# Masked self-attention over sequences of mixed length: waits for older loops moved into skip branches, and GpSimd's casts reading their row masks from the table

## The chip, the cores and the metric

The kernel runs on one NeuronCore of one Trainium2 chip. The metric is the device time of one execution in microseconds. One execution has been recorded by the hardware profiler; all times "from the span's start" below are from that record.

## The reference

Thirty-two sequences of up to 512 tokens (the lengths are drawn between 64 and 511) with 512 features go through one self-attention layer with 8 heads of 64 features. What lies behind a sequence's length stays zero in the output.

```
for b in range(batch):
    seq_len = lengths[b]
    x_b = x[b, :seq_len].copy()
    qkv = np.matmul(x_b, w_qkv)
    q, k, v = np.split(qkv, 3, axis=-1)
    ...
    scores = scale * np.matmul(q, k.transpose(0, 2, 1))
    scores_max = np.max(scores, axis=-1, keepdims=True)
    attn = np.exp(scores - scores_max)
    attn = attn / (np.sum(attn, axis=-1, keepdims=True) + 1e-08)
    out_b = np.matmul(attn, v).transpose(1, 0, 2).reshape(seq_len, dim)
    output[b, :seq_len] = out_b
```

## The kernel before

**Sorting and loops.** The sequences are sorted by length on the chip and taken in 16 pairs, longest first. There is one loop for each padded length N of 512, 448, 384, 352, 320, 288, 256, 224, 192, 160, 128 and 96 (LOOPS). A loop runs over the pairs whose longer member fits N and not the next smaller one; the register end_v says at which pair it stops. A loop with no pair is passed over by the compare-and-branch at its entry (L1477); a loop that has run a pair goes back, or on, at L1497. One pass through a body handles one pair in two *positions*, j = 0 and j = 1, so that the run has 32 positions, 0 to 31.

**A position.** While the attention of one sequence is computed, the next sequence is projected. In position p TensorE does the scores of sequence p (s, L1123), its weighted sums (a, L1207), and the Q, K and V projections of sequence p+1 (q and k L261, v L272). ScalarE takes the exponentials of the scores (L1137) and some copies out of PSUM. VectorE takes the other copies (L1165, L1181), and behind each group of weighted sums three operations: R, the reciprocal of the row sums (L1217, reads PSUM), U, which multiplies it by the row mask in the spare column of v_aug or in the tile queries (L1223, both inputs in SBUF), and O, the division into the output tile (L1226, reads PSUM). O0, O2, O4, O6 are the divisions of the heads from 0, 2, 4, 6 on; in the widest loops there is one for every head.

**Input and masks.** The input of a sequence runs ahead of its projection. In position p SyncE loads x of sequence p+5 in float32 (LD, L1006), and GpSimd casts sequence p+3 to float16 and blanks the rows behind its length (C: one tensor_tensor multiply at L319 for each tile of 128 rows, x times a mask column broadcast along the row). SyncE then transposes that result by DMA (XT, L289) into xT, from which the projections of position p+2 read. The float32 buffers, the float16 buffers and xT are rings of two, taken by parity, so that C of position p writes the buffer that XT of position p-2 reads. The mask for C is made on VectorE: operation M (pair_mask, L968) copies the row of the table alive that belongs to the sequence, at an address from a register, into the tile mask (m_bufs), also a ring of two. Behind M on VectorE stands L (L1044), which writes the spare column of v_aug for the next sequence from alive, and, in loops whose last tile is at most half full, for that tile from a second table, lower. In these loops GpSimd also gathers the half tiles of two sequences (Y, L1066), and at the entry of a loop it may clear columns of kT (E, L1302) or half a tile of v_aug (Z, L1310).

**Order.** The order of the steps in each position is written out by hand in ORDER, in short names: P stands for M and C, D for LD, L, S for scores and exponentials, K, Q, V for projections with their copies (a star puts the copy on ScalarE), A for weighted sums with R, U and O, X for XT. Each engine runs its own part of that list in order, and positions follow one another without a barrier.

**Waits.** plan_waits walks through every chain of loops that can occur (the head, then a loop; a loop u, then a loop v) and gives each operation the waits it needs: a semaphore per operation name, which counts its executions, against a constant or a register. A register named pos, iter or rare grows with each pass; posin, iterin and rarein are set at a loop's entry (L1468 and L1470 to L1475); end_v is worked out in the head from the loops' ends. A wait is an instruction of its own where it doesn't ride on the operation (L1418). A loop that follows on its direct predecessor may need fewer waits than one that follows on a loop further back, when those between have been passed over. In the kernel before these waits stand in the loop's body all the same, and are carried out whether loops were passed over or not; posold is a register that keeps an older entry's value for them.

**The head.** Ahead of the loops stand the sort, the tables, the first two sequences' cast and projections, the weights' casts, and idle matmuls on a tile of ones ("warm") between them.

Of the kernel before, what the change touches and what calls it, by code (L numbers as in the profile page):

```python
# [14 lines left out]
ALU = mybir.AluOpType  # L15
AX = mybir.AxisListType

P = 128
# [17 lines left out]
def plan_waits(head, bodies, entries, rare):  # L36
# [13 lines left out]

    waits = defaultdict(list)
    has = [{op.name for j in range(2) for op in body[j]} for body in bodies]
    shared = set().union(*has)

    def follow(chain):
# [5 lines left out]
        for at, v in enumerate(chain):  # L64
# [10 lines left out]
            for w, j, k, op in todo:  # L75
# [13 lines left out]
                for wait in waits[w, j, k]:  # L89
                    got = [  # L90
                        o
                        for o in seen[wait[1]]
                        if wait[0] in ("last", "entry", "head", "lead")
                        or (wait[0] == "pos" and o["b"] == b - wait[2])
                        or (wait[0] == "iter" and o["b"] // 2 == b // 2 - wait[2])
                        or (wait[0] == "posin" and o["b"] == first - wait[2])
                        or (wait[0] == "posold" and older and o["b"] == first - wait[2])
                        or (wait[0] == "iterin" and o["b"] // 2 == first // 2 - wait[2])
                    ]
                    if got:  # L100
                        learn(got[-1])
# [5 lines left out]
                for o in sorted(needs, key=lambda o: -o["order"]):  # L107
                    if mine[o["by"]] >= o["count"]:
                        continue
                    before = o["b"] < first  # L110
                    if o["entry"]:
                        wait = ("entry", o["name"])
                    elif o["name"] not in shared:
                        wait = ("head", o["name"])
                    elif v == "head":
                        wait = ("lead", o["name"])
                    elif before and o["name"] in rare:
                        wait = ("iterin", o["name"], first // 2 - o["b"] // 2)
                    elif o["name"] in rare:
                        wait = ("iter", o["name"], b // 2 - o["b"] // 2)  # L120
                    elif o["dma"] and before:
                        wait = ("iterin", o["name"], first // 2 - o["b"] // 2)
                    elif o["dma"]:
                        wait = ("iter", o["name"], b // 2 - o["b"] // 2)
                    elif o["name"] not in has[v]:
                        wait = ("last", o["name"])
                    elif before:
                        wait = ("posold" if older else "posin", o["name"], first - o["b"])
                    else:
                        wait = ("pos", o["name"], b - o["b"])  # L130
                    waits[w, j, k].append(wait)
                    learn(o)
                by = op.name if op.dma else op.eng
                count = (seen[by][-1]["count"] if seen[by] else 0) + 1
                after = dict(mine)
# [14 lines left out]
    for v in range(len(bodies)):  # L150
# [1 line left out]
        for u in reversed(range(v)):  # L152
            follow([u, v, v])
        follow(["head", v, v])
    return waits, has


@with_exitstack
def kernel(
# [170 lines left out]
    def before_loops():  # L330
# [280 lines left out]
        fetch("x1.0", 1, 1, 0, 0, NT // 2)  # L611
        fetch("x1.2", 1, 1, 0, NT // 2, NT)

        warm("warm1", ones16, 16, 1, ())

        more = small(
            "more",
# [164 lines left out]
        def twos(source):  # L782
# [50 lines left out]
        )  # L833
        joined("table", four, computed, 20, ("four", "computed"), table)
        op(
            "M",
            "DVE",
            lambda: dve.tensor_scalar(
                out=m_bufs[0], in0=alive[:, 2, :], scalar1=0.0, scalar2=None, op0=ALU.add
            ),  # L840
            ("alive",),
            ("m0",),
        )
        op(
            "L",
            "DVE",
            lambda: dve.tensor_scalar(
# [44 lines left out]

        def casts():
            for t in range(NT):
                last = cast(0, t, nc.gpsimd)
            return last

        op("C", "POOL", casts, ("xn0", "m0"), ("x160", *(f"x160.{t}" for t in range(NT))))
        op("zeros", "POOL", lambda: pool.memset(zeros, 0.0), (), ("zeros",))
        fetch("LD0", 1, 1, 2, 0, NT)  # L900
        op(
# [10 lines left out]
        op("joinPE", "PE", lambda: None, [f"xT1.{t}" for t in range(NT)], [f"bk{k}" for k in (2, 4, 5, 6)])  # L912
        op("joinACT", "ACT", lambda: None, [f"et{e}" for e in range(4)])
        op("joinSP", "SP", lambda: None, ("zeros", "table"))
        op("joinDVE", "DVE", lambda: None, ("lower",), ["m1"])
        op("joinPOOL", "POOL", lambda: None, [f"xT1.{t}" for t in range(NT)], [f"x161.{t}" for t in range(NT)])
        return ops

# [29 lines left out]
    def position(N, j, at, ring):  # L948
# [15 lines left out]
        def op(*args, **kw):  # L964
            ops.append(Op(*args, **kw))

        def pair_mask():
            return nc.vector.tensor_scalar(  # L968
                out=m_bufs[o],
                in0=alive[:, bass.ds(at("DVE") + (j + 3), 1), :].rearrange("p o t -> p (o t)"),  # L970
                scalar1=0.0,
                scalar2=None,
                op0=ALU.add,
            )

        def casts():
            for t in range(n):
                last = cast(o, t, nc.gpsimd)
            return last

        def numbers(pair, handles):
# [265 lines left out]
        for step in steps(N, j):  # L1247
            kind, act = step[0], step.endswith("*")
            num = int(step.strip("*")[1:] or 0)
            if kind == "P":  # L1250
                op("M", "DVE", pair_mask, (), (f"m{o}",))
                op("C", "POOL", casts, (f"xn{o}", f"m{o}"), (f"x16{o}",))
                if half_last and j == 0:
                    for b in (1, 0):
                        op(f"Y{b}", "POOL", lambda b=b: gathered(b), (f"xT{b}",), ("lastT",))
# [61 lines left out]
    def at(eng):  # L1317
        return here[eng]
# [5 lines left out]
    entries = [entry(N) for N in LOOPS]  # L1324
    head = before_loops()
    rare = {"Y0", "Y1", "w", "W0", "W1"}
    waits, has = plan_waits(head, bodies, entries, rare)

    def op_of(v, j, k):
        return head[k] if v == "head" else (entries[v] if j is None else bodies[v][j])[k]  # L1330

    lead = defaultdict(int)
    awaited = set()
    for key, todo in waits.items():
        for wait in todo:
            if wait[0] == "head":
                awaited.add(wait[1])
# [24 lines left out]
    def value_of(v, j, wait):  # L1362
# [5 lines left out]
            return "pos", lead[name] + 1 - wait[2] + j  # L1368
        if wait[0] == "iter":
            return f"iter{unit(name)}", unit(name) * (lead[name] + 1 - wait[2])  # L1370
        if wait[0] in ("posin", "posold"):
            return wait[0], lead[name] + 1 - wait[2]
        if wait[0] == "iterin":
            return f"iterin{unit(name)}", unit(name) * (lead[name] + 1 - wait[2])
        if wait[0] == "lead":
# [5 lines left out]


    raised = {"pos": 2, "rare": 1, "iter16": 16, f"iter{16 * NT}": 16 * NT}
    entered = {"posold": 0, "posin": 2, "rarein": 1, "iterin16": 16, f"iterin{16 * NT}": 16 * NT}

    wanted = defaultdict(set)
    fixed = defaultdict(set)
    for (v, j, k), todo in waits.items():
        op = op_of(v, j, k)
        for wait in todo:  # L1390
            base, amount = value_of(v, j or 0, wait)
            if base:
                wanted[op.eng].add((base, amount))
                if base in entered:
                    fixed[v, op.eng].add((base, amount))
                if base == "posold":
                    wanted[op.eng].add(("posin", amount))
                    fixed[v - 1, op.eng].add(("posin", amount))

    def emit(v, j, k, op):  # L1400
        if not op.skip:
# [27 lines left out]
    with tc.tile_critical():  # L1429
# [32 lines left out]

        for v, N in enumerate(LOOPS):
            for e, eng in EN.items():
                for base, amount in sorted(fixed[v, e], key=lambda f: (f[0] != "posold", f)):
                    reg = regs[e][base, amount]
                    if base == "posold":
                        eng.reg_mov(reg, regs[e]["posin", amount])  # L1468
                        continue
                    eng.reg_mul(reg, rare_pair if base == "rarein" else pair, entered[base])  # L1470
                    eng.reg_add(reg, reg, amount)
            for k, op in enumerate(entries[v]):
                emit(v, None, k, op)
            for e in final:
                EN[e].reg_sub(final[e], of(ends[v], e), 1)  # L1475
            body, after = f"loop_{N}", f"after_{N}"
            nc.br_lt(pair, ends[v], on_true=body, on_false=after)  # L1477
            with nc.body(body):
                hints = {}
# [59 lines left out]
```

## Time and profile before

| what | value |
|---|---|
| median of 3 runs | 343.71 us (343.44 to 344.86) |
| profiled execution | 343.52 us |
| its span, first to last instruction | 341.7 us |
| VectorE's mask copies (L968) | 32, 5.5 us |
| GpSimd's casts (L319) | 85 tiles, 86.3 us |
| TensorE's granted clock, mean | 0.995 |

The profile counts an engine as busy while it executes; register, branch and semaphore instructions are not counted, and appear with a q behind the engine's name (PEq, DVEq; PEldq for TensorE's, in the views by line). In the groups by line, "x" is the count, then come the busy time in us and the mean duration in ns, and after the second bar the engine's idle time just before these instructions with what ended most of it. In views of one line, three numbers divided by slashes are minimum, median and maximum in ns. In the timeline a row has start and duration in us, engine, line, operation, output and input, count, and in brackets the idle time ahead of it. In the chain of work a row has start, length and name. A row of the windows has the stretch, its length, then the busy time and count for each engine, TensorE's clock, the DMA share and GB/s. A matmul's weight load (PEld) is a row of its own.

In the profiled execution the loops' first scores start at these times (us): 512 at 22.2, 448 at 60.8, 384 at 95.9, 352 at 121.8, 320 at 195.6, 288 at 218.9, 256 at 241.9, 224 at 257.1, 192 at 284.9, 160 at 297.3, 128 at 321 (first matmuls at 322.84), 96 at 330.9. Each row of the profile before can be placed in its loop by them.

### The profile page before, as it was taken

To read this page: it belongs to the slowest core of one execution; us is meant where nothing else is said; L and a number is where in the kernel's file an instruction comes from. 1 tells how busy PE (TensorE), PEld (TensorE's weight loads), DVE (VectorE), ACT (ScalarE), POOL (GpSimd) and SP (SyncE) were. 2 spreads that over 40 slices of the span, in tenths; PEclk is the share of its full clock that TensorE was granted. 3 is DMA by queue.
4 is the path that set the end of the run, shared out by engine and by line. 5 is a ranking of instruction groups with operands and counts; after the bars stand their busy time and mean duration, and the time that the engine had idled before them with its cause. 6 is when DMAs were issued, how large, how long until landed. Compare 5 with 4: busy or idle time off the path is not lost.

```text
span 341.7 us, 10763 instructions
## 1 busy us (share of the span) xinstructions
PE 323.0 (95%) x3830; PEld 199.8 (58%) x3830; DVE 217.5 (64%) x660; ACT 262.9 (77%) x414; POOL 103.7 (30%) x147
## 2 busy tenths in 40 slices
PE   6999999999999999999999999899999999898881
PEld 4444545554646556555655656565777776676660
DVE  6676666757666575555565567665776548778673
ACT  5389898897968878888988888688577887686641
POOL 5546040604030231232033043033222344253321
PEclk9999999999999999999999999999999999999998
DMA  6974993574538957948649559869974766696741
GB/s 214 380 272 88 342 192 120 159 276 143 158 59 284 308 160 259 270 138 290 216 146 315 191 156 340 233 225 266 270 244 143 191 170 215 215 159 215 232 141 64
DMA packets 72988, 72.28 MB, mean 212 GB/s; under 512 B 42736, under 2 KB 42736, under 8 KB 72944
## 3 DMA queue, kind: packets, MB, share of 16 engines
q1 hardware_dynamic: 72896, 71.72, 71.1%
q8 instruction: 24, 0.39, 0.4%
q14 instruction: 20, 0.16, 0.1%
q10 hardware_dynamic: 48, 0.00, 0.0%
HBM read 28.32 MB, written 33.55 MB: 181 GB/s over the span
## 4 chain that ended last, share of the span: by engine, by line
PE 89%; DVE 5%; issue 2%; DMA 1%; SPq 0%; DVEq 0%; POOL 0%; POOLq 0%
PE banks L261 37%; PE banks L272 18%; PE banks L1207 17%; PE banks L1123 16%; PE banks L1079 2%; DMA x_nat<-in_x_dram 1%; DVE out_nat L1226 1%; DVE rcp L1223 1%; DVE rcp L1217 1%; DVE v_aug L1181 1%; PE banks L706 0%; DVE v_aug L1044 0%; SPq L585 0%; DVE kT L755 0%; DVE kT L1165 0%
## 5 line engine op out<-in xcount | busy, mean ns | idle before, releaser
L1137 ACT ACTIVATE et<-banks 128x704 f16<-128x704 f32 (+6 forms) x264 | 196.2, 813 | 37.6 <-PE banks L1123 37.1
L261 PE MATMUL banks<-xT,w_r 128*128 128x352 f16 (+11 forms) x1024 | 145.8, 287 | 0.2
L319 POOL TENSOR_TENSOR x<-x_nat,mask 128x512 f16<-128x512 f32 x85 | 86.3, 1041 | 186.7 <-DVE mask L968 180.9
L261 PEld LDWEIGHTS banks<-xT,w_r 128*128 128x128 f16 x1024 | 85.5, 98 | 40.1 <-issue 7.5
L1207 PEld LDWEIGHTS banks<-v_aug,et 128*128 128x128 f16 x1792 | 65.9, 98 | 21.5 <-issue 7.5
L1207 PE MATMUL banks<-v_aug,et 128*128 128x65 f16 x1792 | 73.9, 194 | 1.6 <-DVEq L1408 1.1
L272 PE MATMUL banks<-w_r,xT 128*128 128x512 f16 x284 | 72.3, 380 | 0.8 <-DVE xT L715 0.5
L1123 PE MATMUL banks<-qz,kT 64*128 64x352 f16 (+11 forms) x640 | 62.3, 298 | 7.1 <-DVE out_nat L1226 2.7
L1226 DVE TENSOR_TENSOR out_nat<-banks,rcp 128x256 f32<-128x256 f32 (+1 forms) x136 | 64.1, 471 | 4.6
L1217 DVE RECIPROCAL rcp<-banks 128x4 f32<-128x4 f32 (+1 forms) x136 | 25.0, 184 | 40.1 <-PE banks L1207 38.8
L1123 PEld LDWEIGHTS banks<-qz,kT 64*128 64x128 f16 x640 | 23.0, 94 | 38.9 <-issue 28.4
L1181 DVE CAST v_aug<-banks 128x512 f16<-128x512 f32 x49 | 33.7, 690 | 16.9 <-PE banks L272 16.6
L1165 DVE CAST qz<-banks 128x352 f16<-128x352 f32 (+5 forms) x46 | 26.2, 569 | 28.1 <-PE banks L261 27.7
L272 PEld LDWEIGHTS banks<-w_r,xT 128*128 128x128 f16 x284 | 23.7, 97 | 27.2 <-issue 4.9
L1165 ACT CAST kT<-banks 128x352 f16<-128x352 f32 (+5 forms) x62 | 29.4, 476 | 11.3 <-PE banks L261 10.2
L1165 ACT CAST qz<-banks 128x352 f16<-128x352 f32 (+5 forms) x45 | 21.5, 478 | 7.3 <-PE banks L261 6.0
L1223 DVE TENSOR_TENSOR rcp<-rcp,v_aug 128x4 f32<-128x4 f32 (+1 forms) x108 | 19.6, 182 | 3.7
L1165 DVE CAST kT<-banks 128x512 f16<-128x512 f32 (+4 forms) x29 | 16.9, 588 | 7.6 <-PE banks L261 7.1
L1181 ACT CAST v_aug<-banks 128x512 f16<-128x512 f32 x18 | 10.8, 601 | 5.1 <-PE banks L272 5.1
L1302 POOL MEMSET kT<- 128x128 f16 (+1 forms) x8 | 1.7, 219 | 29.6 <-PE banks L1123 29.5
L968 DVE TENSOR_SCALAR mask<-alive 128x4 f32 x32 | 5.5, 173 | 8.0 <-issue 7.9
L405 PE MATMUL banks<-h_ones 128*128 128x128 f16 (+1 forms) x32 | 5.0, 338 | 2.5 <-POOL h_blank L397 2.5
(80 smaller groups left out, 88.8 us busy)
## 6 DMA issues: line engine op xcount, KB each, us to landing
x_nat<-in_x_dram SPq DMA_DIRECT2D x12, 768.0 KB, 5.5
out_dram<-out_nat SPq DMA_DIRECT2D x12, 768.0 KB, 4.0
x_nat<-in_x_dram SPq DMA_DIRECT2D x14, 512.0 KB, 3.8
x_nat<-in_x_dram SPq DMA_DIRECT2D x7, 1024.0 KB, 7.5
out_dram<-zeros SPq DMA_DIRECT2D x12, 512.0 KB, 5.6
out_dram<-out_nat SPq DMA_DIRECT2D x12, 512.0 KB, 3.0
out_dram<-out_nat SPq DMA_DIRECT2D x4, 1024.0 KB, 4.7
out_dram<-zeros SPq DMA_DIRECT2D x12, 256.0 KB, 5.4
```

The source lines that it names most:

```text
L261: last = nc.tensor.matmul(dst[:, 0:N], w_r[:, c, w0 : w0 + P], xT[:, c, 0:N], start=(c == 0), stop=(c == NC - 1),)
L272: last = nc.tensor.matmul(pv, xT[:, c, t * P : (t + 1) * P], w_r[:, c, 2 * D : 3 * D], start=(c == 0), stop=(c == NC - 1),)
L319: return engine.tensor_tensor(out=x16, in0=x32, in1=live.broadcast_to([P, D]), op=ALU.mult)
L1079: last = nc.tensor.matmul(bank, last_xT[:, c, :], w_r[:, c, 2 * D : 3 * D], start=(c == 0), stop=(c == NC - 1),)
L1123: last = nc.tensor.matmul(psc[par][:, x * n128 : x * n128 + N], kT[r, i, c0 : c0 + P], qz[r, i, 0:N], start=True, stop=True,)
L1137: return nc.scalar.activation(out=et[:, :, x0:x1, 0:N], in_=got.rearrange("p j (x q) -> p j x q", q=n128)[:, :, x0:x1, 0:N], func=AF.Exp, ...
L1165: return copy_on(act)(out=buf[:, ms, 0:N], in_=bank[:, 0 : gm * N].rearrange("p (m q) -> p m q", q=N),)
L1181: return copy_on(act)(out=v_bufs[o][:, t, :, 0:HD], in_=bank.rearrange("p (h d) -> p h d", d=HD))
L1207: last = nc.tensor.matmul(pav[:, g, qt, :], e_bufs[e][:, c0 + qt * P : c0 + (qt + 1) * P], v_aug[:, kt, h, :], start=(kt == 0), stop=(kt = ...
L1217: return nc.vector.reciprocal(out=rcp, in_=pav[:, :, :, HD])
L1223: return nc.vector.tensor_tensor(out=rcp, in0=rcp, in1=rows, op=ALU.mult)
L1226: return nc.vector.tensor_tensor(out=o_t[:, 0:n, h0 * HD : (h0 + heads) * HD].rearrange("p t (g d) -> p g t d", d=HD), in0=pav[:, :, :, 0:HD],
```

## The change

Four things are changed.

1. plan_waits returns a second table, passed_over. A wait that an operation in a loop's body (or entry) needs only if its predecessor loop was passed over (older), and whose producer ran before the loop (before), goes there, under the loop ahead of it and the engine. At that loop's entry, ahead of the branch that enters or passes it, each engine that has such waits compares pair with end_v and carries them out if the loop is about to be passed over (pass_over); otherwise it jumps over them. The register posold is gone; registers that such waits need are set inside the branch.
2. M is gone, in the head and in the bodies. C multiplies by the column of alive itself, at an address from a register of GpSimd, in place of the copied mask. C's dependence on M is gone with it.
3. The head's second group of idle matmuls (warm1) has 30 matmuls in place of 16.
4. joinDVE no longer waits for readers of the mask buffer.

```diff
...
 
 
 
-    waits = defaultdict(list)
+    waits, passed_over = defaultdict(list), defaultdict(list)
     has = [{op.name for j in range(2) for op in body[j]} for body in bodies]
     shared = set().union(*has)
 
...
                         or (wait[0] == "pos" and o["b"] == b - wait[2])
                         or (wait[0] == "iter" and o["b"] // 2 == b // 2 - wait[2])
                         or (wait[0] == "posin" and o["b"] == first - wait[2])
-                        or (wait[0] == "posold" and older and o["b"] == first - wait[2])
                         or (wait[0] == "iterin" and o["b"] // 2 == first // 2 - wait[2])
                     ]
                     if got:
...
                     elif o["name"] not in has[v]:
                         wait = ("last", o["name"])
                     elif before:
-                        wait = ("posold" if older else "posin", o["name"], first - o["b"])
+                        wait = ("posin", o["name"], first - o["b"])
                     else:
                         wait = ("pos", o["name"], b - o["b"])
-                    waits[w, j, k].append(wait)
                     learn(o)
+                    if older and before:
+                        known = passed_over[w - 1, op.eng]
+                        known += [wait] * (wait not in known)
+                    else:
+                        waits[w, j, k].append(wait)
                 by = op.name if op.dma else op.eng
                 count = (seen[by][-1]["count"] if seen[by] else 0) + 1
                 after = dict(mine)
...
         for u in reversed(range(v)):
             follow([u, v, v])
         follow(["head", v, v])
-    return waits, has
+    return waits, passed_over, has
 
 
 @with_exitstack
...
         fetch("x1.0", 1, 1, 0, 0, NT // 2)
         fetch("x1.2", 1, 1, 0, NT // 2, NT)
 
-        warm("warm1", ones16, 16, 1, ())
+        warm("warm1", ones16, 30, 1, ())
 
         more = small(
             "more",
...
         )
         joined("table", four, computed, 20, ("four", "computed"), table)
         op(
-            "M",
-            "DVE",
-            lambda: dve.tensor_scalar(
-                out=m_bufs[0], in0=alive[:, 2, :], scalar1=0.0, scalar2=None, op0=ALU.add
-            ),
-            ("alive",),
-            ("m0",),
-        )
-        op(
             "L",
             "DVE",
             lambda: dve.tensor_scalar(
...
 
         def casts():
             for t in range(NT):
-                last = cast(0, t, nc.gpsimd)
+                last = nc.gpsimd.tensor_tensor(
+                    out=x16_bufs[0][:, t, :],
+                    in0=x_bufs[0][:, t, :],
+                    in1=alive[:, 2, t : t + 1].broadcast_to([P, D]),
+                    op=ALU.mult,
+                )
             return last
 
-        op("C", "POOL", casts, ("xn0", "m0"), ("x160", *(f"x160.{t}" for t in range(NT))))
+        op("C", "POOL", casts, ("xn0", "alive"), ("x160", *(f"x160.{t}" for t in range(NT))))
         op("zeros", "POOL", lambda: pool.memset(zeros, 0.0), (), ("zeros",))
         fetch("LD0", 1, 1, 2, 0, NT)
         op(
...
         op("joinPE", "PE", lambda: None, [f"xT1.{t}" for t in range(NT)], [f"bk{k}" for k in (2, 4, 5, 6)])
         op("joinACT", "ACT", lambda: None, [f"et{e}" for e in range(4)])
         op("joinSP", "SP", lambda: None, ("zeros", "table"))
-        op("joinDVE", "DVE", lambda: None, ("lower",), ["m1"])
+        op("joinDVE", "DVE", lambda: None, ("lower",))
         op("joinPOOL", "POOL", lambda: None, [f"xT1.{t}" for t in range(NT)], [f"x161.{t}" for t in range(NT)])
         return ops
 
...
         def op(*args, **kw):
             ops.append(Op(*args, **kw))
 
-        def pair_mask():
-            return nc.vector.tensor_scalar(
-                out=m_bufs[o],
-                in0=alive[:, bass.ds(at("DVE") + (j + 3), 1), :].rearrange("p o t -> p (o t)"),
-                scalar1=0.0,
-                scalar2=None,
-                op0=ALU.add,
-            )
-
         def casts():
+            rows = alive[:, bass.ds(at("POOL") + (j + 3), 1), :].rearrange("p o t -> p (o t)")
             for t in range(n):
-                last = cast(o, t, nc.gpsimd)
+                last = nc.gpsimd.tensor_tensor(
+                    out=x16_bufs[o][:, t, :],
+                    in0=x_bufs[o][:, t, :],
+                    in1=rows[:, t : t + 1].broadcast_to([P, D]),
+                    op=ALU.mult,
+                )
             return last
 
         def numbers(pair, handles):
...
             kind, act = step[0], step.endswith("*")
             num = int(step.strip("*")[1:] or 0)
             if kind == "P":
-                op("M", "DVE", pair_mask, (), (f"m{o}",))
-                op("C", "POOL", casts, (f"xn{o}", f"m{o}"), (f"x16{o}",))
+                op("C", "POOL", casts, (f"xn{o}",), (f"x16{o}",))
                 if half_last and j == 0:
                     for b in (1, 0):
                         op(f"Y{b}", "POOL", lambda b=b: gathered(b), (f"xT{b}",), ("lastT",))
...
     entries = [entry(N) for N in LOOPS]
     head = before_loops()
     rare = {"Y0", "Y1", "w", "W0", "W1"}
-    waits, has = plan_waits(head, bodies, entries, rare)
+    waits, passed_over, has = plan_waits(head, bodies, entries, rare)
 
     def op_of(v, j, k):
         return head[k] if v == "head" else (entries[v] if j is None else bodies[v][j])[k]
 
     lead = defaultdict(int)
     awaited = set()
-    for key, todo in waits.items():
+    for todo in (*waits.values(), *passed_over.values()):
         for wait in todo:
             if wait[0] == "head":
                 awaited.add(wait[1])
...
             return "pos", lead[name] + 1 - wait[2] + j
         if wait[0] == "iter":
             return f"iter{unit(name)}", unit(name) * (lead[name] + 1 - wait[2])
-        if wait[0] in ("posin", "posold"):
-            return wait[0], lead[name] + 1 - wait[2]
+        if wait[0] == "posin":
+            return "posin", lead[name] + 1 - wait[2]
         if wait[0] == "iterin":
             return f"iterin{unit(name)}", unit(name) * (lead[name] + 1 - wait[2])
         if wait[0] == "lead":
...
 
 
     raised = {"pos": 2, "rare": 1, "iter16": 16, f"iter{16 * NT}": 16 * NT}
-    entered = {"posold": 0, "posin": 2, "rarein": 1, "iterin16": 16, f"iterin{16 * NT}": 16 * NT}
+    entered = {"posin": 2, "rarein": 1, "iterin16": 16, f"iterin{16 * NT}": 16 * NT}
 
     wanted = defaultdict(set)
     fixed = defaultdict(set)
...
                 wanted[op.eng].add((base, amount))
                 if base in entered:
                     fixed[v, op.eng].add((base, amount))
-                if base == "posold":
-                    wanted[op.eng].add(("posin", amount))
-                    fixed[v - 1, op.eng].add(("posin", amount))
+
+    for (v, e), todo in passed_over.items():
+        for wait in todo:
+            base, amount = (None, 1) if wait[0] == "head" else value_of(v, 0, wait)
+            if base:
+                wanted[e].add((base, amount))
+
+    def enter(e, base, amount):
+
+        reg, eng = regs[e][base, amount], EN[e]
+        eng.reg_mul(reg, rare_pair if base == "rarein" else pair, entered[base])
+        eng.reg_add(reg, reg, amount)
+
+    def pass_over(v, e):
+
+        for wait in passed_over[v, e]:
+            if wait[0] == "head":
+                EN[e].wait_ge(*point[wait[1]])
+                continue
+            base, amount = value_of(v, 0, wait)
+            if base in entered:
+                enter(e, base, amount)
+            EN[e].wait_ge(sems[wait[1]], regs[e][base, amount] if base else amount)
+        if passed_over[v, e]:
+            EN[e].sem_inc(passed, 1)
 
     def emit(v, j, k, op):
         if not op.skip:
...
 
         for v, N in enumerate(LOOPS):
             for e, eng in EN.items():
-                for base, amount in sorted(fixed[v, e], key=lambda f: (f[0] != "posold", f)):
-                    reg = regs[e][base, amount]
-                    if base == "posold":
-                        eng.reg_mov(reg, regs[e]["posin", amount])
-                        continue
-                    eng.reg_mul(reg, rare_pair if base == "rarein" else pair, entered[base])
-                    eng.reg_add(reg, reg, amount)
+                for base, amount in sorted(fixed[v, e]):
+                    enter(e, base, amount)
             for k, op in enumerate(entries[v]):
                 emit(v, None, k, op)
             for e in final:
                 EN[e].reg_sub(final[e], of(ends[v], e), 1)
             body, after = f"loop_{N}", f"after_{N}"
+            for e in EN:
+                if passed_over[v, e]:
+                    with EN[e].If_cmp(of(pair, e), of(ends[v], e), "IS_GE"):
+                        pass_over(v, e)
+                    EN[e].end_ifs()
             nc.br_lt(pair, ends[v], on_true=body, on_false=after)
             with nc.body(body):
                 hints = {}
```

## The prediction

> **What bounds the kernel now.** I read the page first: busy times, the chain of work that ended last, and the two groups that the change touches.
>
> ```profile
> PE 323.0 (95%) x3830; PEld 199.8 (58%) x3830; DVE 217.5 (64%) x660; ACT 262.9 (77%) x414; POOL 103.7 (30%) x147
> ...
> PE 89%; DVE 5%; issue 2%; DMA 1%; SPq 0%; DVEq 0%; POOL 0%; POOLq 0%
> ...
> L319 POOL TENSOR_TENSOR x<-x_nat,mask 128x512 f16<-128x512 f32 x85 | 86.3, 1041 | 186.7 <-DVE mask L968 180.9
> ...
> L968 DVE TENSOR_SCALAR mask<-alive 128x4 f32 x32 | 5.5, 173 | 8.0 <-issue 7.9
> ```
>
> TensorE bounds it. GpSimd waits 180.9 us for the mask copies, but it is an engine that is 30% busy and has 0% of the chain, so the end of that wait is worth nothing by itself. The table of busy time by windows says how much there is to win between the first loop's start and the last loops:
>
> ```profile
> 22.20:329.50 307.30, 301.32 (x3648) 187.13 (x3648) 197.76 (x595) 248.94 (x389) 91.81 (x106) 1.00 0.73 211
> ```
>
> 307.30 - 301.32 = 6.0 us of idle TensorE at a clock of 1.00. No matmul goes away, so an edit that shortens waits can win at most these 6 us, and realistically only those that it touches. The profiled run took 343.52 us, its span 341.7 and 1.8 around it; the median of the runs is 343.71, 0.19 higher. I sum against 343.52.
>
> **Which code runs.** The lengths of this draw, sorted and paired, have longest members 502, 446, 363, 351, 343, 323, 310, 260, 246, 223, 216, 164, 143, 134, 101, 79. Every one of the twelve loops gets at least one pair, so none is passed over. The waits that the change puts into branches "for a loop that is passed over" are thus never executed here: what is left is that the loops lose them, and that the branch itself is jumped over, at 11 loop entries on TensorE (all but the last loop), 4 on GpSimd and 1 on ScalarE (counted in the two built kernels).
>
> **Part 1, loop entries on TensorE.** The prices are the sequencer's rows, by line:
>
> ```profile
> L1418 PEldq EVENT_SEMAPHORE  x143: 51/51/1638, 22.1 to 335.7; - x143
> L1407 PEldq COMPARE_BRANCH  x9: 65/176/360, 325.8 to 335.2; - x9
> L1497 PEldq COMPARE_BRANCH  x16: 67/70/231, 60.4 to 336.1; - x16
> ```
>
> L1497 ends a loop: about 0.07 us where it falls through, up to 0.231 where it jumps back. L1407 jumps forward, as the new branch will: median 0.176, at most 0.36. I take 0.25 for a jump with the step behind it: 11 x 0.25 = +2.75 us of sequencer time. A satisfied wait (L1418) takes 0.051; I take 0.10 with its step. Ahead of the first matmul of the twelve loops stand 33 waits before and 9 after: 24 x 0.10 = -2.4. The two nearly cancel, but not place by place: loops 512 to 352 lose 0 or 1 wait each, loops 256 to 96 two to four. What of it reaches the array is only what the sequencer is not ahead of. The chain shows how thin that is at two entries (448 to 384, and 288 to 256):
>
> ```profile
> 95.74 0.14 issue
> ...
> 241.64 0.26 issue
> ```
>
> So the early entries, which gain a jump and lose hardly a wait, should each show 0.1 to 0.25 more: I take +0.7 for 512, 448, 384 and 352 together, +0.2 for 320, 288 and 160, and nothing for 256 to 192. Sum **+0.9**, bounds 0 (all hidden by the sequencer's lead) and +2.75.
>
> One removed wait was not satisfied, at the entry of loop 128 (the timeline, then the chain):
>
> ```profile
> 319.90 0.16 DVE L1223 TENSOR_TENSOR rcp<-rcp,queries 128x4 f32<-128x4 f32 x1
> ...
> 320.89 0.42 DVE L1226 TENSOR_TENSOR out_nat<-banks,rcp 128x256 f32<-128x256 f32 x1
> ...
> 322.00 0.42 DVE L1226 TENSOR_TENSOR out_nat<-banks,rcp 128x256 f32<-128x256 f32 x1
> ...
> 322.84 0.34 PE L1123 MATMUL banks<-qz,kT 64*128 64x128 f16 x6 [1.29 <-issue]
> ```
>
> The first scores wait there for O6, the last division (322.00 + 0.42 = 322.42), and start 0.42 later, after TensorE idled 1.29. In the changed kernel they need only O4 (320.89 + 0.42 = 321.31), which is done before TensorE's own work ends at 321.55; O6 is waited for later, by the projection that takes its bank. Up to -1.29; if the cast below holds the multiply at 319.90, O4 ends about 0.9 later and some -0.4 is left. I take **-0.7**.
>
> **Part 2, the mask copy goes and the casts start earlier.** VectorE loses 32 x 173 ns = 5.5 us, nearly all beside TensorE's work. What matters is when the casts run, since some VectorE operations stand still beside them. The groups by shape, and the line of the multiply:
>
> ```profile
> L1044 DVE TENSOR_SCALAR v_aug<-lower 128x8 f16 x6 | 6.3, 1048 | 0.0
> ...
> L1044 DVE TENSOR_SCALAR v_aug<-alive 128x8 f16 x7 | 1.3, 185 | 0.0
> ...
> L1223 DVE TENSOR_TENSOR rcp<-rcp,v_aug x108: 164/166/891, 31.2 to 336.6; 128x4 f32<-128x4 f32 x68, 128x6 f32<-128x6 f32 x40
> ```
>
> The same shape costs 185 ns, or 1048 ns when it follows the mask copy, for at that moment the cast that waited for the copy starts. The multiply takes 166 ns, and 891 once. Here is that once:
>
> ```profile
> 125.16 2.04 POOL L319 TENSOR_TENSOR x<-x_nat,mask 128x512 f16<-128x512 f32 x2
> ...
> 126.33 0.89 DVE L1223 TENSOR_TENSOR rcp<-rcp,v_aug 128x6 f32<-128x6 f32 x1
> 127.26 0.56 DVE L1226 TENSOR_TENSOR out_nat<-banks,rcp 128x384 f32<-128x384 f32 x1
> ```
>
> It ends with the cast (125.16 + 2.04 = 127.20). Operations that read PSUM (L1226, L1217) are not stretched. So a cast that moves relieves one place and burdens another by up to 0.89 - 0.17 = 0.7 us. Without the copy the cast of position p starts when the transposes issued in position p-2 have landed and GpSimd is free: 1 to 15 us earlier, in most positions over 5. The places, one by one:
>
> ```profile
> 121.36 3.98 SPq L289 DMA_TRANSPOSE xT<-x  x3
> ...
> DMA to landing us min/median/max: 2.3/2.8/7.8
> ```
>
> *352, first position.* The cast that stretches the multiply at 126.33 moves ahead to about 119. The next one needs the last of the transposes shown here, issued near 124.0 and landing at 126.3 or later, so the multiply is past before it starts. TensorE idled 0.11 and 0.44 behind the late division and the V copy after it: **-0.5**.
>
> *320 entry.* The chain runs through VectorE alone here:
>
> ```profile
> 196.89 0.09 DVE mask L968
> ...
> 197.17 1.05 DVE v_aug L1044
> 198.22 0.39 DVE qz L1165
> ...
> 198.65 0.31 PE banks L1123 x2
> ```
>
> The copy (0.17 with its step) goes, and the cast can start once GpSimd's clearing before it is over:
>
> ```profile
> 195.66 0.52 POOL L1310 MEMSET v_aug<- 64x512 f16 x1 [2.80 <-PE banks L1207]
> ```
>
> At 196.2, then, so that its first tile ends near 197.25 and the lower-mask write passes near 197.4 in place of 198.22. TensorE's gap was 0.54: **-0.45**. The entry of loop 192 has the same order: **-0.4**.
>
> *New burdens.* In the third and the fifth position of loop 352 the cast's third tile now covers a multiply that was free:
>
> ```profile
> 153.84 0.17 DVE L1223 TENSOR_TENSOR rcp<-rcp,v_aug 128x6 f32<-128x6 f32 x1
> ...
> 154.52 0.51 DVE L1165 CAST qz<-banks 128x352 f16<-128x352 f32 x1
> ```
>
> 0.5 later, with 0.4 between that Q copy's end and its reader: 2 x 0.12 = **+0.25**. In loop 448 a multiply whose division TensorE waits for with 0.3 to spare: **+0.2** (bounds 0 and 0.6). At the entry of 288 the multiply at 219.02 leads straight to a wait of TensorE:
>
> ```profile
> 219.02 0.17 DVE L1223 TENSOR_TENSOR rcp<-rcp,queries 128x6 f32<-128x6 f32 x1
> ...
> 220.03 0.30 PE L1123 MATMUL banks<-qz,kT 64*128 64x288 f16 x2 [0.84 <-DVE out_nat L1226]
> ```
>
> **+0.2** (0 to 0.4). Loops 256 and 224, two first multiplies within 0.1 us of a cast's reckoned start (one of them the 268.93 below): **+0.3** (0 to 1.0). Loops 192 and 160 have more, but GpSimd gathers first, and the readers have room: 0. The casts read the table at an address from a register, one register instruction each on GpSimd, 30% busy: 0.
>
> *The end.* Nothing hides VectorE here:
>
> ```profile
> 334.78 0.12 DVE mask L968
> ...
> 335.74 0.31 DVE rcp L1223
> ```
>
> The copy leaves the chain (-0.15), and the multiply loses its cast (0.31 to 0.17): **-0.3**.
>
> **Part 3, warm-up matmuls**, 14 more in the head. 32 of them (12 twice as wide) took 5.0 us, 0.11 per 128 columns: at most 1.6 us, in front of two idle stretches:
>
> ```profile
> PE banks L706 <- DVE x L314: 0.7, 1, 0.7
> PE banks L272 <- DVE xT L715: 0.5, 1, 0.5
> ```
>
> 0 to +0.4; I take **+0.1**.
>
> **Sum**: 0.9 - 0.7 - 0.5 - 0.45 - 0.4 + 0.25 + 0.2 + 0.2 + 0.3 - 0.3 + 0.1 = -0.4 us, 343.1; with half of the median's 0.19 above the profiled run, **343.2 us**: no change.
>
> **Rivals.**
> *The jump costs a fetch of code.* VectorE shows such a thing once: its first operation in loop 288 waited 1.5 us for nothing that is shown, against about 0.5 in other entries:
>
> ```profile
> 221.27 0.17 DVE L968 TENSOR_SCALAR mask<-alive 128x4 f32 x1 [1.49 <-issue]
> ```
>
> If each of the 11 jumps did that to TensorE (1.0 each), it would be +11 us, 354. Against it: nine forward branches on TensorE took 0.36 at most. 0.05. [...]
>
> *The casts hold VectorE where TensorE follows closely* (slower). A cast is two to four tiles of 1.04 us back to back; where its start slips by 0.1 to 0.2 us against my reckoning, it covers the first multiply of a group and the delays follow one another: 0.7 us each, less 0.1 to 0.3 of room. It decides where a cast's start comes ahead of the multiply instead of behind it, as with these two (transposes, then multiply):
>
> ```profile
> 268.93 0.17 DVE L1223 TENSOR_TENSOR rcp<-rcp,v_aug 128x4 f32<-128x4 f32 x1
> ```
>
> ```profile
> 316.04 2.54 SPq L289 DMA_TRANSPOSE xT<-x  x2
> ```
>
> The second transposes of the lower row go out near 317.3 and land between 319.6 and 320.1, about where the multiply at 319.90 stands. There are six such places (one in each of loops 256, 224, 192 and 160, two in loop 352). Five of them at 0.6: +3.0, 346.1. Against it: in the two of loop 352 the multiply is ahead by about 0.25 us. 0.22. [...]
>
> *All reliefs, no burden* (faster). -1.3 at loop 128, -0.5, -0.45, -0.4, -0.3, a further 0.3 of the 192 gap, and +0.6 at the entries: -2.6, 340.9. For it: each gap is in the trace. Against: it needs every new neighbourhood to be harmless. 0.24.
>
> **How the numbers follow.** Forecast 0.49, fetch 0.05, burdens 0.22, reliefs 0.24. A measurement here tells from no change what exceeds about 0.5% (1.7 us), so faster 0.24, same 0.49, slower 0.27. The range, 340.8 to 346.4, reaches into both neighbours and leaves the fetch out.
>
> **What would show it.** Right: the lower-mask writes near 0.2 us; the copies' group gone; TensorE idle at the 320, 192 and 128 entries shorter by 0.4 to 1.3, at the 512 to 352 entries longer by 0.1 to 0.25; forward branches near 0.2 us; GpSimd's wait for masks replaced by one for DMA. Wrong: many multiplies near 0.9 us with TensorE waiting for L1226 or a cast behind them; entries longer by 1 us; or a wait that I hold for satisfied that now ends late somewhere else.

## The result and the profile after

The changed kernel takes 347.39 us (median of 5 runs, 346.14 to 347.90) against 343.44 for the kernel before: 1.0102 times as long, interval 1.0074 to 1.0131. It is slower by about 4 us. The forecast was 343.2 (no change); the rival "the casts hold VectorE" had 346.1, and the range ended at 346.4.

The profiled execution took 347.9 us, its span 346.0. First the page of the changed kernel (chain by engine and line, then two groups; U is now L1218, the casts L968):

```profile
PE 83%; DVE 10%; DMA 2%; issue 2%; SPq 1%; ACT 0%; POOL 0%; POOLq 0%; DVEq 0%
...
L968 POOL TENSOR_TENSOR x<-x_nat,alive 128x512 f16<-128x512 f32 x80 | 81.1, 1039 | 126.7 <-DMA xT<-x 63.4
...
L1218 DVE TENSOR_TENSOR rcp<-rcp,v_aug 128x4 f32<-128x4 f32 (+1 forms) x108 | 29.9, 277 | 3.7
```

VectorE's share of the chain went from 5% to 10%. The casts no longer wait for a mask but for the transposes, as foreseen, and the multiply U went from a mean near 180 ns to 277. Its own line, and the write from the lower table in the groups by shape:

```profile
L1218 DVE TENSOR_TENSOR rcp<-rcp,v_aug x108: 165/168/1041, 31.5 to 340.8; 128x4 f32<-128x4 f32 x68, 128x6 f32<-128x6 f32 x40
L1218 DVE TENSOR_TENSOR rcp<-rcp,queries x28: 161/164/849, 87.8 to 325.7; 128x4 f32<-128x4 f32 x20, 128x6 f32<-128x6 f32 x8
```

```profile
L1039 DVE TENSOR_SCALAR v_aug<-lower 128x8 f16 x6 | 1.3, 212 | 0.0
```

So 5.0 us of held writes went (6.3 to 1.3) and held multiplies came: 34 of the 136 took over 230 ns in place of 7, and together 14.4 us more than 170 ns each, in place of 1.6 (sums over all rows of the line). TensorE sits idle 9.5 us in the loops (310.60 - 301.09), where it was 6.0:

```profile
22.40:333.00 310.60, 301.09 (x3647) 186.26 (x3648) 202.34 (x563) 248.90 (x389) 92.44 (x107) 1.00 0.72 208
```

How one hold reaches TensorE, in the second position of loop 352 (timeline):

```profile
141.73 3.03 POOL L968 TENSOR_TENSOR x<-x_nat,alive 128x512 f16<-128x512 f32 x3 [11.41 <-DMA xT<-x]
...
142.79 1.00 DVE L1218 TENSOR_TENSOR rcp<-rcp,v_aug 128x6 f32<-128x6 f32 x1
...
143.82 0.56 DVE L1221 TENSOR_TENSOR out_nat<-banks,rcp 128x384 f32<-128x384 f32 x1
...
144.30 0.51 DVE L1160 CAST qz<-banks 128x352 f16<-128x352 f32 x1
...
144.87 0.32 PE L1118 MATMUL banks<-qz,kT 64*128 64x352 f16 x2 [0.16 <-DVE qz L1160]
```

The cast's first tile ends at about 142.77 (141.73 and a tile's mean of 1.04); the multiply starts 0.02 later, meets the second tile and ends with it, at 143.79. The division, the Q copy and the scores follow one behind the other. And at the entry of loop 224, where the cast starts 0.06 ahead of the multiply:

```profile
257.10 2.04 POOL L968 TENSOR_TENSOR x<-x_nat,alive 128x512 f16<-128x512 f32 x2 [1.29 <-DMA xT<-x]
...
257.16 1.00 DVE L1218 TENSOR_TENSOR rcp<-rcp,v_aug 128x4 f32<-128x4 f32 x1
...
258.19 0.42 DVE L1221 TENSOR_TENSOR out_nat<-banks,rcp 128x256 f32<-128x256 f32 x1
...
258.77 0.45 PE L263 MATMUL banks<-xT,w_r 128*128 128x224 f16 x3 [0.50 <-DVE out_nat L1221]
```

Lining up the matmuls of both kernels one by one shows where the 4.3 us of span come in: +0.3 up to the first scores, +0.2 in loop 512, steps of +0.1 to +0.5 at the entries of 448 to 352, +0.3 in loop 352, +0.5 at the entry of 288, +0.6 at that of 224 and +0.2 in it, +0.8 at that of 192, +0.4 in 192, +0.4, +0.2 and +0.5 in 160, +1.1 in 128 and +0.5 at the entry of 96; and back: -0.5 at the entry of 320, -0.3 in 288, -0.6 in 192, -0.9 at the entry of 128.

### The profile page after: what moved, and what is told of

Its sections match the earlier page's. It is cut to its first block, busy times and chain, and to the rows that moved or that the text cites. A ratio compares the mean times of both kernels' runs of the same rounds, so it can differ in the third digit from the quotient of the medians.

```text
span 346.0 us, 10773 instructions
## 1 busy us (share of the span) xinstructions
PE 323.6 (94%) x3844; PEld 199.4 (58%) x3844; DVE 222.9 (64%) x627; ACT 263.0 (76%) x414; POOL 103.7 (30%) x147
## 4 chain that ended last, share of the span: by engine, by line
PE 83%; DVE 10%; DMA 2%; issue 2%; SPq 1%; ACT 0%; POOL 0%; POOLq 0%; DVEq 0%
PE banks L263 34%; PE banks L274 17%; PE banks L1202 16%; PE banks L1118 15%; DVE rcp L1218 4%; DVE out_nat L1221 3%; PE banks L1074 2%; DMA xT<-x 1%; DVE rcp L1212 1%; DMA x_nat<-in_x_dram 1%; PE banks L708 1%; DVE v_aug L1176 0%; SPq L291 0%; DVE kT L1160 0%; DVE qz L1160 0%
## 5 line engine op out<-in xcount | busy, mean ns | idle before, releaser
L968 POOL TENSOR_TENSOR x<-x_nat,alive 128x512 f16<-128x512 f32 x80 | 81.1, 1039 | 126.7 <-DMA xT<-x 63.4
L1218 DVE TENSOR_TENSOR rcp<-rcp,v_aug 128x4 f32<-128x4 f32 (+1 forms) x108 | 29.9, 277 | 3.7
L1039 DVE TENSOR_SCALAR v_aug<-alive 128x24 f16 (+3 forms) x32 | 7.6, 236 | 5.5 <-issue 5.4
L1061 POOL COPY last_xT<-xT 128x256 f16<-128x256 f16 x12 | 4.8, 397 | 13.5 <-SPq L295 9.1
```

Of the source, the lines that this page charges most:

```text
L968: last = nc.gpsimd.tensor_tensor(out=x16_bufs[o][:, t, :], in0=x_bufs[o][:, t, :], in1=rows[:, t : t + 1].broadcast_to([P, D]), op=ALU.mult,)
L1039: return nc.vector.tensor_scalar(out=v_bufs[o][:, t0:t1, :, HD], in0=table[:, bass.ds(at("DVE") + (j + 1), 1), t0:t1] .rearrange("p o t -> ...
L1218: return nc.vector.tensor_tensor(out=rcp, in0=rcp, in1=rows, op=ALU.mult)
```

## The experiments

**Theory A**: the casts, now earlier, hold U, and TensorE waits for what follows U. **Rival B**: the jumps at the loop entries cost it. **Rival C**: something else that comes with earlier casts (transposes, traffic, SyncE's order).

**1. Which part? (e1_waits, e2_masks)** Each half of the change alone. For e1_waits the mask copies come back:

```diff
+                op("M", "DVE", pair_mask, (), (f"m{o}",))
-                op("C", "POOL", casts, (f"xn{o}",), (f"x16{o}",))
+                op("C", "POOL", casts, (f"xn{o}", f"m{o}"), (f"x16{o}",))
```

> The changed kernel with the mask copies put back (M on VectorE, casts waiting for them), so that only the waits and the 30 warm-up matmuls are new. If the earlier casts cost the time by holding U on VectorE: 343.5 to 344.5, at most +1 for the jumps and the warm-up, and U (the multiply by the row mask) back at 166 ns save one or two of them. If the jumps at the loop entries cost it: 346 to 347.5, with U as before.

Measured: 344.41 us against 343.43, ratio 1.0021 (1.0009 to 1.0034).

e2_masks is the kernel before with the same three lines the other way round (and the casts reading alive):

> The kernel before with only the mask copies taken out (casts read the table, start as soon as the transposes two positions back have landed); waits and warm-up as before. If the earlier casts cost the time: 346 to 347, U's mean near 270 ns. If the jumps do: 343 to 343.7.

Measured: 346.36 us, ratio 1.0075 (1.0044 to 1.0105). The parts add up: 0.21% and 0.75% against 1.02%. Three quarters belong to the casts.

**2. Same code on TensorE, casts later (e3_gated, the "gated kernel" below).** In the changed kernel L moves ahead of C in the list, and C waits for it (cut):

```diff
             if kind == "P":
-                op("C", "POOL", casts, (f"xn{o}",), (f"x16{o}",))
+                op("L", ...)                                  # as it stood at "L"
+                op("C", "POOL", casts, (f"xn{o}", f"vl{o}"), (f"x16{o}",))
```

> The changed kernel, except that each cast waits for L, the write of the spare column on VectorE at the start of the same position, so that the casts start about where they did before, but behind L and not beside it. If the earlier casts cost the time: 342.5 to 343.8, with all writes from the table lower near 0.2 us (they took 1.05 before) and U as before. If the jumps or the reading of the table by GpSimd cost it: 346 to 347.

Measured: 343.25 us, ratio 0.9989 (0.9977 to 1.0001). In the loops TensorE runs the very same instructions as in the changed kernel, the 11 jumps among them (in the head one semaphore instruction less); only the casts' start differs, and 4.1 us are gone (347.39 - 343.25). So rival B cannot be the main cause. The multiply's line and the lower writes of this kernel:

```profile
L1218 DVE TENSOR_TENSOR rcp<-rcp,v_aug x108: 165/166/594, 31.3 to 336.6; 128x4 f32<-128x4 f32 x68, 128x6 f32<-128x6 f32 x40
...
L1039 DVE TENSOR_SCALAR v_aug<-lower 128x8 f16 x6 | 1.1, 186 | 0.0
```

That GpSimd reads the table and not a copy cost nothing: a cast tile took 1040 ns on average, 1041 in the kernel before.

**3. Is it the hold, or something else with early casts? (e6_after_noU, e7_before_noU)** U is taken out of both kernels, which then leave the rows behind a sequence's length unmasked:

```diff
-            op(f"U{h0}", "DVE", only_live, (f"r{k}", whose), (f"r{k}",))
```

> The changed kernel without U, the multiply of the reciprocals by the row mask: rows behind a sequence's length are left unmasked. To be compared with the kernel before without U. If held U cost the time, the difference between the two falls from +4.0 us to +1.2 or less (the jumps and what is left at the loop entries). If something else that comes with the earlier casts does, it stays at +3 or more.

> The kernel before without U (rows behind a sequence's length unmasked), as the base for the changed kernel without U. U stands in VectorE's chain of R, U and O at the few places where TensorE waits for O: 341.5 to 343.2, in both theories.

Measured: 341.85 us and 342.30 us, ratios to the kernel before 0.9948 (0.9931 to 0.9966) and 0.9950 (0.9934 to 0.9966). Without U the change no longer costs time. Part of this is the head, which took 1.2 us longer in the second kernel's profiled execution; from the first loop to the end the change costs 0.3 us there, in place of 4.0 with U. Rival C falls.

**4. Does the hold last as long as the cast instruction? (e5_half, e5_quarter)**

```diff
-                last = nc.gpsimd.tensor_tensor(out=x16_bufs[o][:, t, :], ...)
+                for d in range(0, D, D // 2):                 # D // 4 for the quarters
+                    last = nc.gpsimd.tensor_tensor(out=x16_bufs[o][:, t, d : d + D // 2], ...)
```

> The changed kernel with each cast tile of 512 columns done as two instructions of 256 columns. If U waits until the cast instruction that is running has ended, the longest hold falls from about 1.0 to about 0.5 us, and about half of the 4 us by which the changed kernel is slower than the gated one goes: 345.0 to 346.0. If the casts hurt by anything else that comes with their earlier start (the transposes, SyncE's order, DMA traffic): 347 to 348, with U held as long as before.

Measured: 345.16 us, ratio 1.0046 (1.0030 to 1.0062), as theory A expected. The longest hold fell from 1041 to 620 ns, a half tile's mean being 612 (groups, then U's line):

```profile
L969 POOL TENSOR_TENSOR x<-x_nat,alive 128x256 f16<-128x256 f32 x160 | 92.7, 612 | 121.5 <-DMA xT<-x 58.2 <-SPq L295 54.7 <-DMA x_nat<-in_x_dram 5.8
```

```profile
L1219 DVE TENSOR_TENSOR rcp<-rcp,v_aug x108: 164/168/620, 31.6 to 337.3; 128x4 f32<-128x4 f32 x68, 128x6 f32<-128x6 f32 x40
```

Over half of the loss went (1.0102 to 1.0046), with about as many multiplies held as before the halving (30 and 34).

> The changed kernel with each cast tile of 512 columns done as four instructions of 128 columns. If the hold is the rest of the running cast instruction, the step from half to quarter tiles is worth half of that from whole to half tiles: 344.0 to 344.8. If the halves were faster for another reason, or if the casts' longer total keeps VectorE out: 345 or more.

Inconclusive: the four runs took 344.21, 345.99, 352.06 and 352.07 us (granted clock 0.995, 0.994, 0.983 and 0.983), too far apart for a ratio. U's longest hold in the profiled one (345.99) was 1837 ns, across five cast instructions of about 0.40 us, so that "until the running instruction ends" does not always hold for quarters; why is open:

```profile
L1219 DVE TENSOR_TENSOR rcp<-rcp,v_aug x108: 165/168/1837, 31.8 to 338.3; 128x4 f32<-128x4 f32 x68, 128x6 f32<-128x6 f32 x40
```

**5. What do the jumps cost? (e4_nobranch, e8_gated_nobranch)** The branch is left out with the waits in it, in the changed and in the gated kernel, which are then right only for lengths that pass over no loop:

```diff
-            for e in EN:
-                if passed_over[v, e]:
-                    with EN[e].If_cmp(of(pair, e), of(ends[v], e), "IS_GE"):
-                        pass_over(v, e)
-                    EN[e].end_ifs()
```

> The changed kernel without the branches at the loop entries (the waits in them are left out altogether; no loop is passed over in this draw, so they would not be executed). If the earlier casts cost the time: the jumps are worth 0.5 to 1 us, 346.3 to 346.9. If the jumps do: 343.3 to 344.3.

> The gated kernel with the new waits, without the branches at the loop entries. If the jumps cost what the run without them showed on top of the changed kernel (1 to 1.5 us): 341.8 to 342.3. If most of that was a chance of the casts' places: 342.8 to 343.3.

Measured: 345.70 us, ratio 1.0068 (1.0042 to 1.0094), and 340.82 us, ratio 0.9910 (0.9884 to 0.9937). The first lies between its two ranges, the second below both. So the branches cost 1.7 us on the changed kernel and 2.4 on the gated one, more than theory A said. Lined up, the gated pair shows 0.15 to 0.4 at most entries from 448 to 224, and 1.0 at that of 192. The branch's line in the changed kernel, and the one entry that shows more than a jump (192, timeline):

```profile
L1490 PEldq COMPARE_BRANCH  x11: 206/207/342, 22.2 to 324.4; - x11
```

```profile
286.73 0.41 PE L1202 MATMUL banks<-v_aug,et 128*128 128x65 f16 x8
...
287.89 0.38 PE L274 MATMUL banks<-w_r,xT 128*128 128x512 f16 x1 [0.75 <-issue]
```

TensorE waits 0.75 us there for nothing that the profile shows. The same stretch (0.75 to 0.82 us) stands in e1_waits, e3_gated, both kernels of experiment 4 and e6_after_noU, all with the branches, and in neither kernel of this experiment.

**6. Is that the place of the code? (e10_padded)**

```diff
+        spaced("PE", 24)
         warm("warm0", ones16, 12, 2, ("ones",))
```

> The gated kernel with 24 more instructions (semaphore increments) on TensorE's sequencer ahead of the head's first warm-up matmuls, which shifts all of TensorE's code behind them. TensorE's sequencer is silent for about 0.85 us at the entry of loop 192 in every kernel with the branches and in none without. If that is the place of the code (a fetch), the silence goes from there or turns up at another entry. If it is a wait that the changed kernel has there, it stays. The time: within 1 us of 343.25 in both.

Measured: 346.27 us, ratio 1.0064 (1.0045 to 1.0082). The time missed the expectation, since the 24 instructions made the head's first matmul 3.5 us late (6.03 for 2.53) and the first scores 4.3; from there on the padded kernel keeps step with the gated one, within 0.3 us at any one place, except that the stretch at the entry of 192 is 0.78 us shorter, and its row has no idle time:

```profile
288.06 0.41 PE L1203 MATMUL banks<-v_aug,et 128*128 128x65 f16 x8
...
288.52 1.02 PE L274 MATMUL banks<-w_r,xT 128*128 128x512 f16 x4
```

The waits there are the same; the code's place differs, and the time, by about 4 us. The time is hardly the cause, since the stretch stood anywhere from 284.97 to 287.89 in the six kernels that have it. So with this one padding the stretch went as the code's place changed; that a fetch stands behind it is not shown.

**7. A version that beats both (g2_gated_oldwaits, g3_gated_half).** The kernel before, without mask copies, casts waiting for L; then with half tiles too.

> The kernel before (its waits and its 16 warm-up matmuls) with the mask copies out and each cast waiting for L at the start of its position. If held VectorE writes and the jumps are two separate costs, this has neither and keeps the relief of the lower-table writes: 342.0 to 342.9, under both kernels. If the gated kernel's 343.25 hides no cost of the jumps: 343.2 to 343.5.

> The gated kernel with the waits of the kernel before and cast tiles in two instructions of 256 columns each. Few U are held there, so halving the hold is worth little: 342.6 to 343.0. If the casts' longer total matters: 343.2 or more.

Measured: 343.03 us, ratio 0.9977 (0.9965 to 0.9990), and 342.20 us, ratio 0.9960 (0.9946 to 0.9974). The first lies between its two ranges, the second below both of its own. Both are faster than the kernel before, by 0.2% and 0.4%; the intervals overlap, so that the halves' own share is not settled. The three gated kernels also price the waits: 343.03 us with the old waits, 343.25 with the branches in their place, 340.82 with neither. Within their intervals, the branches cost what they save.

## Why the prediction was wrong, point by point

- **New burdens: the step that failed.** The prediction summed them to 0.25 + 0.2 + 0.2 + 0.3 = +0.95 us. Measured, between two kernels with the same TensorE code in the loops: +4.1 (experiment 2), and 0.3 or less without U (3). The mechanism was named rightly, and as a rival with its price; what failed is the size of this term. Lined up place by place, the changed kernel falls behind the gated one (the profiled pair, 4.6 us by the last matmul):

| place | predicted | measured |
|---|---|---|
| 448, one multiply | +0.2 | 0 |
| 352, third and fifth position | +0.25 | 0 (held 0.67 and 0.66 us) |
| 288, entry | +0.2 | +0.6 |
| 256 and 224 | +0.3 | +0.9, all in 224 |
| 192 and 160 | 0 | +1.5 |
| 512; 352, entry and second position; 96, entry | no term | +0.25; +0.5; +0.4 |

  The first position of 352 (+0.4) is the relief of the next point. The largest miss is the term put at 0, because "GpSimd gathers first, and the readers have room". Three of the six casts there ran ahead of the gather, as the one at 311.07 that holds the multiply below; those behind it still held multiplies (at 292.72 and 304.98, for 0.84 and 0.70 us); and the readers had no room, as in loop 160 (the changed kernel, then the same scores in the kernel before):

```profile
311.27 0.85 DVE L1218 TENSOR_TENSOR rcp<-rcp,queries 128x4 f32<-128x4 f32 x1
...
314.38 0.45 PE L1118 MATMUL banks<-qz,kT 64*128 64x160 f16 x8 [1.46 <-DVE out_nat L1221]
```

```profile
310.56 0.45 PE L1123 MATMUL banks<-qz,kT 64*128 64x160 f16 x8 [0.93 <-DVE out_nat L1226]
```

  Behind this stands that reckoned starts were used as if they were exact, while every delay of TensorE moves a multiply against the casts. With whole tiles the hold was a saw-tooth here: a multiply that started 0.08 us before a tile's end took 166 ns (at 68.30), one 0.39 us before it 415 ns (at 41.83), one just behind a tile's start 1041 ns (at 120.32). The second position of loop 352 came out at 1.0 for 0.02 us. 34 multiplies were held where the prediction priced about six.
- **The relief at 126.33 (-0.5)**: not had. The multiply there came later together with TensorE's delay, fell into the next cast, and was held for 0.80 us (127.56 to 128.35); matmuls there came closer by 0.1 only. The gated kernel, where no cast meets it, has the relief: -0.45.
- **The 320 entry (-0.45)**: right, -0.53. **The 192 entry (-0.4)**: the write was free and -0.62 came, but behind +0.85 at the same entry, most of it the silent stretch.
- **Entries (+0.9, bounds 0 and 2.75)**: about right as a balance. The half of the change with the waits alone costs 0.21%, 0.7 us, and its matmuls fall behind by 0.14, 0.18 and 0.26 us at the entries of 448, 384 and 352. A jump took 0.207 as priced (0.25 with its step). What the fetch rival priced at eleven entries showed at one, the silent stretch; that it is a fetch is not shown.
- **Loop 128 (-0.7)**: won and given back (-0.92 at the entry, then +1.08). Without a hold the gated kernel wins 1.36 at this entry and loses 1.51 a position later. Its chain there:

```profile
320.94 0.02 issue
320.95 0.02 SPq L1436
320.97 0.05 issue
321.02 1.20 SPq L291
322.22 0.05 issue
322.27 3.97 DMA xT<-x
326.24 0.05 issue
326.29 0.73 PE banks L263 x10
```

  The transposes for the next projection can be issued only when the values' projection (ended 320.94) has read their buffer, and the last lands at 326.24. The relief, at the loop's first scores, comes after that point and cannot bring them forward. The prediction did not ask what was late next: TensorE came earlier to a transfer that did not.
- **The end (-0.3)**: half of it, -0.14. **Warm-up (+0.1)**: not settled. Once the first scores are through, e1_waits, the gated and the changed kernel, all with 30, stand at -0.01, +0.13 and +0.32 us against the kernel before.
- **Who holds whom**: in the changed kernel the 26 multiplies U that took over 400 ns ended 17 to 26 ns behind the end of a cast's tile. The halved tiles agree (1041 to 620 ns); the 1837 ns beside quarters are longer than one instruction. The divisions, which read PSUM, took no longer beside a cast (at most 558 ns) than elsewhere (559). A cast held by a multiply does not show: the cast tiles of the changed kernel took 1034 to 1045 ns.

## What to carry to other kernels

A wait of an idle engine can be a lock that keeps it out of the way of another, as the casts' wait was here. Before removing it, ask where its work will land, and price that as a distribution: with a hold that jumped from 0 to about 0.9 us at each tile's end, as here (multiplies of 166 to 1041 ns), an estimated start is worth nothing below its own error, and the number of neighbours counts more than the named cases. And a branch that avoids satisfied waits at a loop's entry is not free: here it was no cheaper than they were (343.25 against 343.03 us).

## What the runs showed that was not expected

- A cast of 128x256 took 612 ns where 128x512 took 1039, so that the halves lengthened the casts by 18%, and the changed kernel was faster with them all the same.
- TensorE stood silent for 0.75 us behind one loop entry's branch, and no longer did with 24 more instructions far ahead of it.
- The same jump took 0.207 us on TensorE's sequencer and 0.050 on GpSimd's and ScalarE's (the branch's line again):

```profile
L1490 POOLq COMPARE_BRANCH  x4: 50/50/50, 67.7 to 317.1; - x4
L1490 ACTq COMPARE_BRANCH  x1: 50/50/50, 242.1 to 242.1; - x1
```
